# A two-layer recurrent and attention trunk: another order of the last feed-forward outputs and of the attention's blocks, with packed weights

## The chip, the cores and the metric

The kernel runs on one core of a Trainium2 chip. The time is the device time of one execution in microseconds (us). Three runs of the kernel before gave a median of 1279.37 us, from 1278.56 to 1281.68. Engines go by the names of the profile: PE (matrix products), DVE (VectorE), ACT (ScalarE), POOL (GpSimd) and SP (SyncE, which issues nearly all transfers).

## What is computed

One inference step of a trunk with two layers, over 512 prompt tokens and 64 sample tokens (8 sequences of 8), width 1024, feed-forward width 2816, all in fp32. Layer 0 is a gated recurrence, layer 1 a sliding-window attention with sinks; keys and values are computed once between them. Cut to what matters:

```python
def trunk(x, c, p0, conv_bufs, h0s, k_prev, v_prev, params):
    ...
    for l in range(DEPTH):
        sh1, sc1, g1, sh2, sc2, g2 = ada_mod(c, ada_w[l], ada_b[l], 6)
        h = modulate(rms_norm(x, norm_g[l, 0]), sh1, sc1)
        if l < N_A_LAYERS:
            out, nbuf, h_last = recurrent_block(h, rnn_w_in[l], rnn_conv_w[l], ...)
        else:
            q = apply_partial_rope((h @ attn_w_q[j]).reshape(B, T, N_HEADS, HEAD_DIM), pos)
            out = sliding_sink_attention(q, k_all, v_all, attn_sinks[j], p0) @ attn_w_o[j]
        x = x + g1[:, None, :] * out
        h = modulate(rms_norm(x, norm_g[l, 1]), sh2, sc2)
        x = x + g2[:, None, :] * swiglu(h, ffn_w_in[l], ffn_w_out[l])
        if l == N_A_LAYERS - 1:
            kv_shift, kv_scale = ada_mod(c, kv_ada_w, kv_ada_b, 2)
            hk = modulate(rms_norm(x, kv_norm_g), kv_shift, kv_scale)
            kv = (hk @ w_kv).reshape(B, T, 2, N_KV_HEADS, HEAD_DIM)
            ...
    y = rms_norm(x, final_g)

# in recurrent_block / rg_lru: the gates, one 128x256 block for each 128 channels
g = jnp.einsum('btnc,ncd->btnd', xb, gate_w) + gate_b
```

## The kernel before

**Halves and products.** The tokens are cut into two halves, A and B in the order strings, h = 0 and 1 in the code: 256 prompt tokens and 32 sample tokens each, so HC = 288 columns (with gaps for the convolution, CW = 300). The stream of each half stays on chip as `x[0]`, `x[1]` (x0, x1 in the profile), the normalised operand of its products as `h` (h0x, h1x). Each fp32 product is made of three fp32r matmuls for each 128x128 block of weights: high part of the weights by high and by low part of the operand, and low part of the weights by high part (`product`). A matmul takes 288 columns.

**Weights.** A `Unit` is the weights of one 128-column output. SP loads it into a `raw` slot (four of 128x1024), and `convert` makes two `wh` slots of it: ACT copies the high part, DVE subtracts it from `raw` for the low part. There are ten `wh` slots, so five units at a time. `drop` gives a unit's slots back when both halves have used it (`left` counts down from 2).

**Layer 0.** The string RNN orders input products (x, y) and gates (g0 to g7), and half B runs behind half A. `gates` (L1043 on) splits the convolved channel block `sl` into a high part `ta` (ACT, COPY, shown as CAST) and a low part `tb` (L1049, on POOL), then does three matmuls of 300 columns for each of the two gate units into banks `mm`, and a chain of tanh, exp, sqrt and a scan on ACT, DVE and POOL follows. All weights of the modulations are multiplied in small steps strewn between (`ada`).

**Feed-forward.** `ffn` computes the 22 blocks of 128 middle channels in GROUPS of 6, 6, 6 and 4, and after each group adds that group's share of the output to the stream: `out` multiplies the group by one 128-column output m for one half, and `residual` adds it (a SCALAR_TENSOR_TENSOR for the prompt, and small operations for the samples), and after the last group squares it for the next norm. For the last group `emit` runs half B behind half A by LEAD outputs:

```python
                lead = LEAD if k == len(GROUPS) - 1 else 0
                for j in range(KC + lead):
                    for h, m in ((0, j), (1, j - lead)):
                        if 0 <= m < KC:
                            out(k, m, h)
```

When a half's eighth output is done, `after(h)` is recorded: in layer 0 the sum of squares over the partitions (six matmuls of one column into a bank, with `small` and `acc`), the inverse root (`tst`, then back over the columns into `acc`), and the normed and modulated operand `h` for keys and values; in layer 1 the final norm and the output.

**Keys, values, queries.** Between the layers stand four products for keys and values (`kvjobs`, m = 0 to 3), first all four for half A, then all four for half B. `kv_done` follows each half's fourth: it modulates the operand again for the queries, and for half B first converts two query units.

**Attention.** The string ATT sets the order of the jobs in layer 1: q, a, o are a query product, one attention chunk (two heads) over the half's 256 prompt tokens and an output product; s is one sample sequence, f ends a half. Its last letter is the half. A chunk's scores, softmax, transposes and products with the values are small PE instructions, with DVE, ACT and POOL between them; a query or output product is 24 matmuls.

**The order of instructions.** All of this is only recorded, each operation with a priority (its place in the record, moved by a few `early` biases). `schedule` then builds the order of every engine by a greedy simulation with estimated costs and delays, and the program is written out in that order. So a change of one job moves rows elsewhere too. As all operations are written from one line, all instructions bear L447, and the profile tells them apart by their tiles.

Of the kernel before, what the change touches and what calls it, by code (L numbers as in the profile page):

```python
# [16 lines left out]
ALU = mybir.AluOpType  # L17
AX = mybir.AxisListType

P = 128  # L20
D = 1024
KC = D // P
# [5 lines left out]
HC = 288  # L28
CW = 300
# [1 line left out]
EPS = 1e-6  # L31
SLOT = 304
LAG = 7
LEAD = 4
NHI = 5
ADA, ADA2 = 1.6, 0.95
AB = 4
# [10 lines left out]
MQ = "4 V VVG SSSV VG"  # L48
# [1 line left out]
WIN = 600  # L50

RNN = "x0 x1 x2 g0 g1 x3 y0 y1 x4 g2 g3 x5 y2 x6 y3 g4 g5 x7 y4 y5 g6 g7 y7 y6"
ATT = ("q0A q1A a0A q0B q2A a1A q1B a0B q3A a2A q2B a1B q4A a3A q3B a2B q5A a4A q4B a3B q6A a5A q5B a4B q7A a6A s0A q6B a5B s1A "
       "a7A s2A q7B s3A s0B a6B fA s1B o0A s2B a7B s3B o1A fB o2A")
LOOK = {"PE": 24, "DVE": 24, "ACT": 24, "POOL": 24, "SP": 24}
NRAW = 4
NSL, NTA, NTB, NTD = 37, 7, 8, 4
# [2 lines left out]
SH1, SC1, G1, SH2, SC2, G2 = range(6)  # L60
KVSH, KVSC = 6, 7
L1 = 8
# [411 lines left out]
def trunk_kernel(ctx, tc, a):  # L474
# [93 lines left out]

    xt = [None] * 5

    ALL = slice(0, P)

    def x_load(t):
        xt[t] = regs()
# [346 lines left out]
    def modulated_h(h, gsc, gsh, how, xn=None, known=False):  # L921
        H[h] = hkind[h](F32R)
        modulated(h, gsc, gsh, how, xn=xn, known=known)
# [6 lines left out]
    class Unit:  # L930
        def __init__(self, kc, srcs):
            self.kc, self.srcs, self.raw, self.hi, self.lo = kc, srcs, None, None, None
            self.left = 2

    units = []
    nload, nconv = [0], [0]
# [2 lines left out]
    def load_more(upto=NRAW):  # L939
        while nload[0] < len(units) and nload[0] - nconv[0] < upto:  # L940
            u = units[nload[0]]
            u.raw = raws()
            t = u.raw.f[:, 0 : u.kc * P].rearrange("p (k n) -> p k n", n=P)
            for rows, ks, cols, src in u.srcs:
                Q.dma_start(t[rows, ks, cols], src)
            nload[0] += 1
# [21 lines left out]
    def unit_cols(w, c0, k0=0, kc=KC):  # L968
        src = w[k0 * P : (k0 + kc) * P, c0 : c0 + P].rearrange("(k p) n -> p k n", p=P)
        u = Unit(kc, [(ALL, slice(0, kc), ALL, src)])  # L970
        units.append(u)
        return u

    def product(o, u, ops, first=True, last=True):
        n = u.kc
        hi, lo = u.hi.r, u.lo.r
        for k in range(n):
            xh, xl = ops[k]
            ks = slice(k * P, (k + 1) * P)
            T.matmul(o, hi[:, ks], xh, start=(first and k == 0), stop=False)  # L980
            T.matmul(o, hi[:, ks], xl, start=False, stop=False)
            T.matmul(o, lo[:, ks], xh, start=False, stop=(last and k == n - 1))
# [60 lines left out]
    def gates(c):  # L1043
        def run(h):
            s1 = RN[h][c]
            xc = s1.f[:, 0:CW]
            xh, xl = ta(F32R), tb(F32R)
            S.copy(xh.r[:, 0:CW], xc)
            G.tensor_tensor(xl.r[:, 0:CW], xc, xh.f[:, 0:CW], ALU.subtract)  # L1049
            ks = slice(c * P, (c + 1) * P)  # L1050
            os_ = []
            for u in ug:
# [116 lines left out]
    def ffn(l, g, after):  # L1169
# [24 lines left out]
        f0 = 0  # L1194
        for n in GROUPS:
            blocks.append([(unit_cols(wi, f * P), unit_cols(wi, DFF + f * P)) for f in range(max(f0, PLAIN), f0 + n)])
            outs.append((f0, [unit_cols(wo, m * P, f0, n) for m in range(KC)]))
            f0 += n
        pairs_ = [None] * PLAIN + [b for bs in blocks for b in bs]
        W = {}  # L1200
# [49 lines left out]
        def queue():  # L1250
            for k, bs in enumerate(blocks):
                for i in range(max(PLAIN, sum(GROUPS[:k])), sum(GROUPS[: k + 1])):
                    st = steps(i)
                    if i == PLAIN:
                        nxt = steps(i + 1)
                        for s_, names in ((st, ("11", "12")), (nxt, ("11", "12")), (st, ("22", "S1", "S2", "S3", "S4")), (nxt, ("22", "S1", "S2", "S3", "S4"))):
                            for n in names:
                                todo.append((1, s_[n]))
                    elif i > PLAIN + 1:
                        for n in ("11", "22", "S1", "S2", "12", "S3", "S4"):  # L1260
                            todo.append((1, st[n]))
                for _ in outs[k][1]:
                    todo.append((2, convert))

        def pump(want=lambda: True):
# [73 lines left out]
        def out(k, m, h):  # L1339
            f0, us = outs[k]  # L1340
            n, u = GROUPS[k], us[m]
            pump(lambda: u.hi is not None)
            o = ps()
            product(o[:, 0:HC], u, [(mid[h][f][0].r[:, 0:HC], mid[h][f][1].r[:, 0:HC]) for f in range(f0, f0 + n)])
            last = k == len(GROUPS) - 1
            residual(h, o, m, g, last)
            if last and l == 1:
                final_chunk(h, m)
            drop(u)
            pump()  # L1350
            if m == KC - 1:
                for f in range(f0, f0 + n):
                    for s_ in mid[h][f]:
                        s_.done()
                if last:
                    after(h)
# [143 lines left out]
        return f  # L1500

    def kv_done(h):
        if h == 1:
            convert()
            convert()
        modulated_h(h, L1 + SC1, L1 + SH1, MQ, XN[h], True)

    for m in range(4):
        linear(unit_cols(a["w_kv"], m * P), hops, evac_k(m) if m < 2 else evac_v(m - 2), kv_done if m == 3 else None)


    kvjobs, jobs = jobs, []
# [476 lines left out]
```

## Time and profile before

| what | value |
| --- | --- |
| median of the three runs | 1279.37 us |
| profiled execution | 1278.79 us |
| its span | 1277.0 us |
| DMA moved | 165.40 MB, 130 GB/s |
| POOL | 267.8 us (21%), 558 instructions |

The profiled execution is one run; its span is the time from its first to its last instruction, and 1.8 us lie around it. A busy PE is one that has a matmul running; weight loads (PEld) overlap with it. A windows row gives, for a stretch, each engine's busy time and number of instructions, the clock that PE was granted (1.00 is full) and the share and rate of the DMA. A timeline row gives the start in us and the length of a run of like instructions, and in brackets the idle time ahead of it on its engine, with what ended that.

### The profile page before, as it was taken

How to read it: one execution, taken by the hardware profiler on the slowest of the kernel's cores; microseconds unless marked ns; L12 is line 12 of the kernel's file. 1: busy time of each engine (PE TensorE's matmuls, PEld its weight loads, DVE VectorE, ACT ScalarE, POOL GpSimd, SP SyncE). 2: the span in 40 equal slices, each digit the busy share in tenths (PEclk: the TensorE clock that was granted, in tenths of full speed). 3: DMA queues.
4: the chain of work that ended last, by engine and by line, in shares of the span. 5: the costliest groups of instructions: out<-in, count | busy, mean ns of one | idle time of the engine just before them, and what ended most of it. 6: DMA issues, size and time to landing. Idle time of an engine off the chain costs nothing.

```text
span 1277.0 us, 25350 instructions
## 1 busy us (share of the span) xinstructions
PE 1246.2 (98%) x9532; PEld 1171.9 (92%) x9532; DVE 918.3 (72%) x2275; ACT 668.4 (52%) x1508; POOL 267.8 (21%) x558
## 2 busy tenths in 40 slices
PE   7999999999999999999989999999999999999997
PEld 5788899899999899899988987899999999999997
DVE  6988785895587468657579787448956965875767
ACT  4789873753255235414467678438543541552443
POOL 3476630100100011110133435100001001001012
PEclk9999999999999999999999999899999999999999
DMA  9956454535456654554342321233241342233222
GB/s 305 332 162 215 158 166 149 170 92 174 147 153 193 183 163 155 173 174 149 100 99 48 60 76 50 66 99 112 75 124 55 95 116 82 74 103 90 80 87 75
DMA packets 223982, 165.40 MB, mean 130 GB/s; under 512 B 23758, under 2 KB 209066, under 8 KB 223827
## 3 DMA queue, kind: packets, MB, share of 16 engines
q1 hardware_dynamic: 223410, 163.45, 42.5%
q8 instruction: 75, 1.23, 0.4%
q14 instruction: 49, 0.39, 0.1%
q0 software_dynamic: 448, 0.32, 0.1%
HBM read 160.85 MB, written 4.87 MB: 130 GB/s over the span
## 4 chain that ended last, share of the span: by engine, by line
PE 88%; DVE 7%; ACT 3%; issue 1%; POOL 0%; DMA 0%; ACTq 0%; SPq 0%; DVEq 0%; POOLq 0%
PE mm L447 84%; PE ada L447 4%; DVE sl L447 2%; DVE ta L447 1%; DVE wh L447 1%; DVE h L447 1%; ACT ta L447 1%; ACT L447 1%; DVE tb L447 1%; ACT h L447 1%; ACT sl L447 0%; ACT wh L447 0%; ACT tb L447 0%; DVE raw L447 0%; DVE td L447 0%
## 5 line engine op out<-in xcount | busy, mean ns | idle before, releaser
L447 PE MATMUL mm<-h,wh 128*128 128x288 f32 x4128 | 597.3, 298 | 8.7 <-ACT h L447 3.6
L447 PEld LDWEIGHTS mm<-h,wh 128*128 128x128 f32 x4128 | 561.8, 189 | 29.8 <-issue 10.4
L447 PE MATMUL mm<-sl,wh 128*128 128x288 f32 x3218 | 460.2, 296 | 0.8 <-ACT ta L447 0.8
L447 ACT CAST wh<-raw 128x512 fp32r<-128x512 f32 (+2 forms) x388 | 270.6, 710 | 357.3 <-PE mm L447 217.1
L447 PEld LDWEIGHTS mm<-sl,wh 128*128 128x128 f32 x3218 | 436.2, 188 | 8.9 <-issue 6.7
L447 DVE TENSOR_TENSOR wh<-raw,wh 128x512 fp32r<-128x512 f32 (+2 forms) x388 | 310.6, 812 | 59.2 <-ACT wh L447 57.1
L447 DVE SCALAR_TENSOR_TENSOR x<-mm,mods,x 128x256 f32<-128x256 f32 x160 | 77.1, 482 | 141.9 <-PE mm L447 141.7
L447 POOL TENSOR_TENSOR td<-td,td 128x288 f32<-128x288 f32 x38 | 35.6, 936 | 476.3 <-ACT td L447 468.2
L447 POOL TENSOR_TENSOR x<-x,ta 128x32 f32<-128x32 f32 x152 | 56.0, 368 | 343.2 <-DVE ta L447 343.1
L447 PE MATMUL mm<-tb,wh 128*128 128x288 f32 (+1 forms) x488 | 88.2, 296 | 2.6 <-POOL sl L447 1.6
L447 PEld LDWEIGHTS mm<-tb,wh 128*128 128x128 f32 x488 | 72.4, 188 | 4.5 <-POOL sl L447 1.9
L447 ACT COPY td<-mm 128x288 f32<-128x288 f32 (+2 forms) x140 | 48.7, 363 | 38.7 <-PE mm L447 18.7
L447 DVE TENSOR_TENSOR raw<-raw,raw 128x512 f32<-128x512 f32 x76 | 61.4, 808 | 0.9
L447 PE MATMUL mm<-ta,wh 128*128 128x288 f32 (+1 forms) x254 | 56.0, 298 | 0.0
L447 DVE TENSOR_TENSOR td<-mm,td 128x288 f32<-128x288 f32 x76 | 34.6, 455 | 27.6 <-PE mm L447 27.3
L447 DVE TENSOR_TENSOR raw<-raw 128x512 f32<-128x512 f32 x76 | 52.1, 687 | 1.1
L447 ACT ACTIVATE ta<-x 128x288 f32<-128x288 f32 x56 | 24.8, 444 | 51.6 <-POOL x L447 48.5
L447 PE MATMUL ada<-reg,cz 128*32 128x512 f32 (+1 forms) x448 | 50.3, 553 | 0.3
L447 PEld LDWEIGHTS mm<-ta,wh 128*128 128x128 f32 x254 | 41.5, 188 | 1.7 <-ACT wh L447 0.8
L447 ACT ACTIVATE ta<-ta,stat 128x256 f32<-128x256 f32 (+2 forms) x72 | 32.2, 471 | 17.3 <-DVE stat L447 17.2
L447 DVE TENSOR_TENSOR acc<-acc,ta 128x288 f32<-128x288 f32 x54 | 24.5, 453 | 11.3 <-ACT ta L447 11.3
L447 ACT ACT_TABLE_LOAD x24 | 30.8, 1283 | 3.4 <-DMA raw<-in_c_sample_dram 3.1
(202 smaller groups left out, 1212.7 us busy)
## 6 DMA issues: line engine op xcount, KB each, us to landing
raw<-in_ffn_w_in_dram SPq DMA_DIRECT2D x88, 512.0 KB
reg<-in_ada_w_dram SPq DMA_DIRECT2D x80, 512.0 KB
raw<-in_ffn_w_out_dram SPq DMA_DIRECT2D x48, 384.0 KB
raw<-in_rnn_w_in_dram SPq DMA_DIRECT2D x16, 512.0 KB
reg<-in_kv_ada_w_dram SPq DMA_DIRECT2D x16, 512.0 KB
wh<-in_ada_w_dram SPq DMA_DIRECT2D x24, 256.0 KB
raw<-in_rnn_w_out_dram SPq DMA_DIRECT2D x8, 512.0 KB
raw<-in_ffn_w_out_dram SPq DMA_DIRECT2D x16, 256.0 KB
```

The lines of the kernel that those rows point to most:

```text
L447: self.rec.add(eng, lambda: getattr(obj, name)(*map(real, args), **{k: real(v) for k, v in kw.items()}), cost, outs, ins, func, lat, port, ...
```

## The change

It has five parts. LEAD goes from 4 to 8, in both layers: the last group's eight outputs are all done for half A, then all for half B. The last group's weights (four blocks of 128 rows for an output) are packed by two outputs: `unit_two` loads four blocks of 256 columns into one `raw` slot, `product` picks the half of each block with `col`, and a unit is dropped after four uses; so eight units of 128x512 become four of 128x1024 in each layer. The low part in `gates` is subtracted on DVE instead of POOL (16 instructions). The query weights are converted after the second and the third key and value product of half B, one each, instead of two after the fourth. And ATT is another order of the same jobs. The matmuls are the same ones.

```diff
--- before
+++ changed
-LEAD = 4
+LEAD = 8
...
-ATT = ("q0A q1A a0A q0B q2A a1A q1B a0B q3A a2A q2B a1B q4A a3A q3B a2B q5A a4A q4B a3B q6A a5A q5B a4B q7A a6A s0A q6B a5B s1A "
-       "a7A s2A q7B s3A s0B a6B fA s1B o0A s2B a7B s3B o1A fB o2A")
+ATT = ("q0A a0A q1A q2A q0B a1A q1B a0B a2A q3A q2B a1B a3A q3B q4A q4B a2B q5A a4A a3B q6A a5A q5B a4B "
+       "q7A a6A q6B a5B s0A s1A a7A s2A s3A q7B s0B a6B fA a7B o0A s1B s2B o1A s3B o2A fB")
...
-    ALL = slice(0, P)
+    ALL, ALL2 = slice(0, P), slice(0, 2 * P)
...
             self.kc, self.srcs, self.raw, self.hi, self.lo = kc, srcs, None, None, None
-            self.left = 2
+            self.left, self.width = 2, P
...
-            t = u.raw.f[:, 0 : u.kc * P].rearrange("p (k n) -> p k n", n=P)
+            t = u.raw.f[:, 0 : u.kc * P].rearrange("p (k n) -> p k n", n=u.width)
...
-    def product(o, u, ops, first=True, last=True):
-        n = u.kc
+    def unit_two(w, c0, k0, kc):
+
+        src = w[k0 * P : (k0 + kc) * P, c0 : c0 + 2 * P].rearrange("(k p) n -> p k n", p=P)
+        u = Unit(2 * kc, [(ALL, slice(0, kc), ALL2, src)])
+        u.left, u.width = 4, 2 * P
+        units.append(u)
+        return u
+
+    def product(o, u, ops, first=True, last=True, col=0):
+        n = u.kc * P // u.width
         hi, lo = u.hi.r, u.lo.r
         for k in range(n):
             xh, xl = ops[k]
-            ks = slice(k * P, (k + 1) * P)
+            ks = slice(k * u.width + col, k * u.width + col + P)
...
             S.copy(xh.r[:, 0:CW], xc)
-            G.tensor_tensor(xl.r[:, 0:CW], xc, xh.f[:, 0:CW], ALU.subtract)
+            V.tensor_tensor(xl.r[:, 0:CW], xc, xh.f[:, 0:CW], ALU.subtract)
...
-            outs.append((f0, [unit_cols(wo, m * P, f0, n) for m in range(KC)]))
+            if n <= 4:
+                two = [unit_two(wo, m * P, f0, n) for m in range(0, KC, 2)]
+                outs.append((f0, [two[m // 2] for m in range(KC)]))
+            else:
+                outs.append((f0, [unit_cols(wo, m * P, f0, n) for m in range(KC)]))
...
-                for _ in outs[k][1]:
+                for _ in {id(u) for u in outs[k][1]}:
                     todo.append((2, convert))
...
-            product(o[:, 0:HC], u, [...])
+            product(o[:, 0:HC], u, [...], col=P * (m % 2) if u.width > P else 0)
...
     def kv_done(h):
+        modulated_h(h, L1 + SC1, L1 + SH1, MQ, XN[h], True)
+
+    def ahead_q(h):
         if h == 1:
             convert()
-            convert()
-        modulated_h(h, L1 + SC1, L1 + SH1, MQ, XN[h], True)
 
     for m in range(4):
-        linear(unit_cols(a["w_kv"], m * P), hops, evac_k(m) if m < 2 else evac_v(m - 2), kv_done if m == 3 else None)
+        linear(unit_cols(a["w_kv"], m * P), hops, evac_k(m) if m < 2 else evac_v(m - 2), (None, ahead_q, ahead_q, kv_done)[m])
```

**The gates on PE, layer 0.** The first place is PE where half A's block 6 and its neighbours are done: `mm74` and `mm75` are the two gate banks of one block, `ta63` its high part, `tb47` its low part, `wh19` and `wh21` the high weights, and `h11` the operand of half B's input product. Before:

```order
L447 MATMUL mm74_2127<-ta63_1848,wh19_719 128x300
L447 MATMUL mm74_2127<-ta63_1848,wh20_819 128x300
L447 MATMUL mm75_2132<-ta63_1848,wh21_775 128x300
L447 MATMUL mm75_2132<-ta63_1848,wh22_857 128x300
L447 MATMUL mm76_2139<-h11_441,wh39_1835 128x288 x2
L447 MATMUL mm76_2139<-h11_441,wh40_1851 128x288
```

Eighteen rows of the `h11` product and of another block's gates stand between, and then:

```order
L447 MATMUL mm79_2198<-ta67_2084,wh19_719 128x300
L447 MATMUL mm79_2198<-ta67_2084,wh20_819 128x300
L447 MATMUL mm74_2127<-tb47_2184,wh19_719 128x300
L447 MATMUL mm75_2132<-tb47_2184,wh21_775 128x300
L447 MATMUL mm80_2208<-ta67_2084,wh21_775 128x300
L447 MATMUL mm80_2208<-ta67_2084,wh22_857 128x300
```

With the change:

```order
L447 MATMUL mm74_2129<-ta63_1855,wh19_719 128x300
L447 MATMUL mm74_2129<-ta63_1855,wh20_819 128x300
L447 MATMUL mm74_2129<-tb47_1878,wh19_719 128x300
L447 MATMUL mm75_2137<-ta63_1855,wh21_775 128x300
L447 MATMUL mm75_2137<-ta63_1855,wh22_857 128x300
L447 MATMUL mm75_2137<-tb47_1878,wh21_775 128x300
L447 MATMUL mm76_2147<-h11_441,wh39_1840 128x288 x2
L447 MATMUL mm76_2147<-h11_441,wh40_1861 128x288
```

The matmuls with the low part `tb47` stood 24 and 23 rows behind the last with the high part; now they follow them at once, and the banks' product is complete before the next input product.

**The half norm on DVE, after layer 0's feed-forward.** Here `x0` and `x1` are the streams of the two halves, `mm` the outputs' banks, `tst0` the sums for half A's norm, `acc0` its inverse root, and `sl` and `tb` begin its operand for keys and values. Before:

```order
L447 TENSOR_SCALAR tst0_71<-mm249_8333 128x2
L447 TENSOR_SCALAR tst0_71<-mm249_8333 32x1
L447 SCALAR_TENSOR_TENSOR x1_65<-mm253_8319,mods_68,x1_65 128x256
L447 TENSOR_TENSOR acc1_70<-acc1_70,ta249_8343 128x288
L447 TENSOR_TENSOR ta250_8363<-mm253_8319,mods_68 128x32
L447 SCALAR_TENSOR_TENSOR x1_65<-mm254_8348,mods_68,x1_65 128x256
L447 TENSOR_TENSOR ta252_8387<-mm254_8348,mods_68 128x32
L447 TENSOR_TENSOR sl213_8395<-x0_64,acc0_69 128x128
L447 TENSOR_TENSOR sl205_8400<-x0_64,acc0_69 128x256
L447 TENSOR_TENSOR tb67_8405<-sl213_8395,mods_68 128x128
L447 TENSOR_TENSOR sl206_8407<-x0_64,acc0_69 128x256
```

With the change:

```order
L447 TENSOR_SCALAR tst0_71<-mm246_8234 128x2
L447 TENSOR_SCALAR tst0_71<-mm246_8234 32x1
L447 SCALAR_TENSOR_TENSOR x1_65<-mm249_8220,mods_68,x1_65 128x256
L447 TENSOR_TENSOR ta242_8253<-mm249_8220,mods_68 128x32
L447 TENSOR_TENSOR acc1_70<-acc1_70,ta243_8262 128x288
L447 TENSOR_TENSOR sl213_8273<-x0_64,acc0_69 128x128
L447 TENSOR_TENSOR sl205_8276<-x0_64,acc0_69 128x256
L447 TENSOR_TENSOR tb67_8281<-sl213_8273,mods_68 128x128
L447 TENSOR_TENSOR sl206_8286<-x0_64,acc0_69 128x256
L447 TENSOR_TENSOR tb67_8281<-tb67_8281,mods_68 128x128
L447 TENSOR_TENSOR sl208_8295<-x0_64,acc0_69 128x256
```

The first rows of half A's norm (`sl213`) stood behind the seventh of half B's eight outputs (mm254); now they stand behind its second (mm249), and the other six, from mm250 on, follow the norm.

**The end of the attention on PE.** Here `td` and `wh277` (`wh269`) are the last sample products of half B, `mm368` their bank; `h05` and `h15` are the operands of the output products for halves A and B, `mm400` and `mm402` (before) or `mm400` (changed) banks of half A and `mm399` on of half B; `ada392` is a chunk's product with the values. Before:

```order
L447 MATMUL ada392_10851<-td120_10759,sl224_8648 64x128 x2
L447 MATMUL ada392_10851<-td121_10761,sl225_8876 64x128 x2
L447 MATMUL ada392_10851<-td122_10768,sl225_8876 64x128 x2
L447 MATMUL ada392_10851<-td123_10772,sl226_8813 64x128 x2
L447 MATMUL mm402_10866<-h05_10059,wh308_10795 128x288 x2
L447 MATMUL mm368_10549<-td124_10869,reg109_9632 128x64 x2
L447 MATMUL mm368_10549<-wh277_9769,reg107_7879 128x256 x2
L447 MATMUL mm399_10886<-h15_10319,wh300_9903 128x288
L447 MATMUL mm401_10888<-h15_10319,wh302_9968 128x288
L447 MATMUL mm403_10890<-h15_10319,wh304_10133 128x288
L447 MATMUL mm405_10892<-h15_10319,wh306_10356 128x288
L447 MATMUL mm407_10895<-h15_10319,wh308_10795 128x288
```

With the change:

```order
L447 MATMUL mm368_10588<-td123_10797,reg109_9686 128x64 x2
L447 MATMUL mm368_10588<-td124_10808,reg109_9686 128x64 x2
L447 MATMUL mm368_10588<-wh269_9720,reg107_7879 128x256 x2
L447 MATMUL mm400_10792<-h05_10033,wh299_10583 128x288
L447 MATMUL mm400_10792<-h05_10033,wh298_10533 128x288 x2
L447 MATMUL mm400_10792<-h05_10033,wh299_10583 128x288
L447 MATMUL mm400_10792<-h05_10033,wh298_10533 128x288 x2
L447 MATMUL mm400_10792<-h05_10033,wh299_10583 128x288
L447 MATMUL mm400_10792<-h05_10033,wh298_10533 128x288 x2
L447 MATMUL mm400_10792<-h05_10033,wh299_10583 128x288
L447 MATMUL mm399_10843<-h15_10346,wh292_9780 128x288
L447 MATMUL mm400_10792<-h05_10033,wh298_10533 128x288 x2
```

Between the last sample product and the first matmul with `h15` stood nothing; now ten matmuls of half A's output (mm400) stand there.

2 lines of the change are left out of this document (1 added, 1 removed).

## The prediction

> **What bounds the kernel now.** I read the page's busy shares first, then its chain of work, then stretches of 32 us.
>
> ```profile
> PE 1246.2 (98%) x9532; PEld 1171.9 (92%) x9532; DVE 918.3 (72%) x2275; ACT 668.4 (52%) x1508; POOL 267.8 (21%) x558
> PE 88%; DVE 7%; ACT 3%; issue 1%; POOL 0%; DMA 0%; ACTq 0%; SPq 0%; DVEq 0%; POOLq 0%
> ```
>
> TensorE has a matmul running for 98% of the span and carries 88% of the chain that ended last; the other engines carry it where PE waits for them. The change leaves the matmuls alone, so all it can win is PE's idle time and PE's slow time.
>
> ```profile
> 448.00:480.00 32.00, 32.00 (x245) 30.40 (x244) 21.74 (x44) 10.76 (x21) 4.21 (x8) 1.00 0.52 164
> ...
> 640.00:672.00 32.00, 28.56 (x205) 26.80 (x204) 24.92 (x69) 21.83 (x47) 12.57 (x19) 1.00 0.43 100
> 672.00:704.00 32.00, 29.43 (x213) 27.91 (x213) 28.72 (x77) 22.70 (x56) 13.09 (x16) 1.00 0.29 59
> ...
> 768.00:800.00 32.00, 29.57 (x249) 23.05 (x249) 23.33 (x110) 26.51 (x99) 18.98 (x46) 1.00 0.20 60
> 800.00:832.00 32.00, 29.58 (x208) 27.11 (x209) 13.88 (x57) 12.30 (x42) 3.34 (x9) 0.84 0.25 72
> ...
> 1248.00:1277.00 29.00, 22.03 (x169) 20.57 (x167) 21.27 (x80) 9.61 (x19) 6.24 (x14) 0.90 0.24 83
> sum 1277.00, PE 1246.23 PEld 1171.95 DVE 918.27 ACT 668.37 POOL 267.79; mean PE 31.16 PEld 29.30 DVE 22.96 ACT 16.71 POOL 6.69
> ```
>
> The sum leaves 1277.0 - 1246.2 = 30.8 us of PE idle. A full stretch, 448 to 480, does 245 matmuls in 32 us: 0.131 us each, my price for a row of PE. Three stretches that the change touches are not full: keys and values (640 to 704) lack 3.4 + 2.6 = 6.0 us, and the attention's end (768 to 832) 2.4 + 2.4 = 4.8 us, with a clock of 0.84 in its last row. The tail lacks 7.0 us, and its last residual still waits for the same last matmul, so I leave it at nothing.
>
> **Gates: the low part goes from POOL to DVE.** These are the timeline rows around two late gates, and the groups of the operation moved and of its nearest kin on DVE.
>
> ```profile
> 152.07 1.05 POOL L447 COPY ta<-shT 128x4 f32<-128x4 f32 x1 [0.90 <-DVE ta L447]
> ...
> 153.94 0.81 POOL L447 TENSOR_TENSOR tb<-sl,ta 128x300 fp32r<-128x300 f32 x1
> ...
> 154.80 0.55 PE L447 MATMUL mm<-tb,wh 128*128 128x300 f32 x2 [1.64 <-POOL sl L447]
> ...
> 157.57 0.55 PE L447 MATMUL mm<-tb,wh 128*128 128x300 f32 x2 [0.37 <-POOL tb L447]
> ```
>
> ```profile
> L447 POOL TENSOR_TENSOR tb<-sl,ta 128x300 fp32r<-128x300 f32 x16 | 14.4, 910 | 0.0
> L447 DVE TENSOR_TENSOR sl<-sl,tb 128x300 f32<-128x300 f32 x16 | 8.4, 529 | 0.7 <-POOL tb L447 0.7
> ```
>
> PE stood 1.64 + 0.37 = 2.0 us for two low parts, as POOL worked through the chain of the gate before. In the new order on PE the low part follows the high part at once and stands on DVE, ahead of that chain. I take both waits as gone: **-2.0**. What DVE gets is 16 subtractions at 0.529 us, 8.5 us. They lie beside PE's products, as DVE has room:
>
> ```profile
> 64.00:160.00 96.00, 93.98 (x704) 83.68 (x703) 80.14 (x153) 84.01 (x158) 63.15 (x140) 1.00 0.55 178
> ```
>
> In these 96 us DVE is busy for 80.1; with 8.5 more it is at 88.6, or 92%. What is queued behind each subtraction on DVE is a weight's low part or a scan, and PE waits for the first. Bounds: at best also the 0.81 us that stand ahead of the first output product, -2.8; at worst all 8.5 us reach PE, 8.5 - 2.0 = +6.5. I stay near the best end, since the moved instruction ends earlier than before.
>
> ```profile
> 150.80 0.37 POOL L447 COPY ta<-shT 128x4 f32<-128x4 f32 x1 [1.99 <-DVE ta L447]
> ...
> 151.85 1.22 DVE L447 TENSOR_TENSOR wh<-raw,wh 128x1024 fp32r<-128x1024 f32 x1
> ```
>
> The same small copy on POOL takes 0.37 us alone and 1.05 us beside a DVE subtraction of 1.22 us. The Trainium skill, "SBUF — State Buffer", section "Who interferes with whom", says why: a DVE operation with two SBUF inputs takes a port pair that it shares with GpSimd, for its whole length. By that rule the move ends 16 such meetings of subtractions and opens 16 others with POOL's gate chain; the sum would stay where it is.
>
> **Keys and values: LEAD 8, and query weights earlier.** The waits of the two stretches, from the timeline:
>
> ```profile
> 658.44 1.70 PE L447 MATMUL mm<-h,wh 128*128 128x288 f32 x10 [1.08 <-ACT h L447]
> 660.29 0.66 PE L447 MATMUL mm<-h,wh 128*128 128x288 f32 x3
> ...
> 662.13 1.33 PE L447 MATMUL mm<-h,wh 128*128 128x288 f32 x8 [1.18 <-POOL h L447]
> ...
> 664.50 2.51 PE L447 MATMUL mm<-h,wh 128*128 128x288 f32 x16 [1.03 <-DVE wh L447]
> 666.84 0.69 PE L447 MATMUL mm<-small,acc 128*128 128x1 f32 x6
> ...
> 697.12 8.09 PE L447 MATMUL mm<-h,wh 128*128 128x288 f32 x59 [1.44 <-DVE wh L447]
> ```
>
> Half A's products wait 1.08 + 1.18 us for pieces of the normed operand h, and some 0.15 between (660.29). In the new order half A's sum of squares stands 46 rows earlier on PE, 46 x 0.131 = 6.0 us, while its first product stays where it was: there are now 76 rows between, for 33. DVE starts the norm behind half B's second output instead of its seventh. So these waits of 2.4 us go. What is late next is the low part of the second unit: 1.03 us of wait before, and now it stands behind six of half B's residuals.
>
> ```profile
> L447 DVE SCALAR_TENSOR_TENSOR x<-mm,mods,x 128x256 f32<-128x256 f32 x160 | 77.1, 482 | 141.9 <-PE mm L447 141.7
> ```
>
> ```profile
> 656.32 0.70 DVE L447 TENSOR_TENSOR sl<-x,acc 128x128 f32<-128x128 f32 x2
> ...
> 661.03 0.45 DVE L447 TENSOR_TENSOR acc<-acc,ta 128x288 f32<-128x288 f32 x1
> ...
> 661.80 0.18 DVE L447 TENSOR_TENSOR ta<-mm,mods 128x32 f32<-128x32 f32 x1
> ...
> 662.68 1.76 DVE L447 TENSOR_TENSOR wh<-raw,wh 128x1024 fp32r<-128x1024 f32 x1
> 664.37 0.41 DVE L447 TENSOR_TENSOR h<-tb,h 128x256 fp32r<-128x256 f32 x1
> ```
>
> The norm took DVE from 656.32 to 664.8, with a low part of 1.76 and one residual (0.48 + 0.18 + 0.45) among it; moved up by 6.0 it begins near 650.3, and without those its first 18 rows end near 656. The six residuals (6 x 0.48, 6 x 0.18, and three additions of squares of 0.45 ahead of the low part: 5.3, a little less as they overlap) end near 661, and the low part of 1.2 to 1.8 us near 662.3; PE, 25 rows into keys and values that begin at 657.4, wants it at 660.7. I take a wait of 1.5, 0.5 more than before. Half B's own waits are what is left, 6.0 - 2.4 - 1.0 - 1.4 = 1.1; its sum of squares comes earlier on PE and on DVE alike, so they stand. The 1.44 us at 697.12 are a wait for a query unit's low part: with two units converted ahead, in a stretch where DVE is otherwise busy 28.7 of 32 us, I take 1.0 of it. Sum -2.4 + 0.5 - 1.0 = **-2.9**. At best all 6.0 go. At worst the six unread outputs hold all six banks, and PE's next product, wanted at 657.4, waits for the first residual behind the norm; if the 18 rows end at 658.4 only, that is 1.0 + 0.48 + 0.18, some 1.7 us more: -1.2.
>
> **Attention: another order.** Here are four rows of the timeline, the last two from the stretch before the first, and three windows of 4 us.
>
> ```profile
> 806.93 3.46 PE L447 MATMUL mm<-h,wh 128*128 128x288 f32 x24
> ...
> 827.76 4.51 PE L447 MATMUL mm<-h,wh 128*128 128x288 f32 x22 [1.59 <-ACT h L447]
> ```
>
> ```profile
> 799.92 1.01 PE L447 MATMUL mm<-ident,reg 128*128 128x128 f32 x4 [0.56 <-PE mm L447]
> 801.24 0.48 PE L447 MATMUL mm<-ident,ta 128*128 128x128 f32 x1 [0.32 <-ACT tb L447]
> ```
>
> ```profile
> 800.00:804.00 4.00, 3.62 (x18) 2.75 (x20) 1.55 (x5) 2.51 (x11) 0.19 (x1) 0.50 0.55 157
> 804.00:808.00 4.00, 4.00 (x34) 3.54 (x32) 2.90 (x17) 1.62 (x7) 0.45 (x1) 0.64 0.46 132
> 828.00:832.00 4.00, 4.00 (x22) 4.00 (x23) 0.82 (x2) 0.00 (x0) 0.00 (x0) 0.66 0.45 131
> ```
>
> At 827.76 PE had waited 1.59 us for half B's operand, with nothing between the last sample product and that operand's first use. Now ten matmuls stand there: 10 x 0.131 = 1.3 of it is covered, and more follow interleaved, so I take -1.6 with the rest. The 22 matmuls behind took 4.51 us, for 22 x 0.131 = 2.9: the clock was 0.66 in that window. With the gap gone I take that as gone too, -1.6. Before 806.93 the order held 88 rows without a large product; now it holds 49, so 44% of the idle 2.4 us of 768 to 800, -1.0. The dip at 800 I keep. Sum **-4.2**. At best all idle of 768 to 832 and both dips (2.3 + 1.6) go, -8.7; at worst the waits move and nothing is gained: 0. SP's loads bear on that end: the fourth sample of a half loads its cache into the first one's buffer, and in the new order 25 rows of PE stand between the two uses, for 49. The rest of SP's queue keeps its order, at a DMA share of 0.2.
>
> The half clock at 800 came with gaps of 0.56 and 0.32 us and none longer. The Trainium skill, "TensorE: Matmul & The Clock Gate", section "What's actually happening", lets the clock fall only after an idle window of about 3.4 us; by it neither dip comes from one gap of 1.6 us, and covering the gap need not remove the dip.
>
> **Packing.** Each layer's eight conversions become four:
>
> ```profile
> L447 DVE TENSOR_TENSOR wh<-raw,wh 128x512 fp32r<-128x512 f32 x282 | 191.2, 694 | 46.7 <-ACT wh L447 45.3
> L447 DVE TENSOR_TENSOR wh<-raw,wh 128x1024 fp32r<-128x1024 f32 x58 | 72.7, 1255 | 9.3 <-ACT wh L447 8.7 <-issue 0.3
> ```
>
> That is 8 x 0.694 - 4 x 1.255 = 0.5 us of DVE in each layer, beside full PE windows: nothing. It holds eight of ten slots until half B is done; if that cover fails, the price is the wait for the second unit counted above.
>
> **Sum.** -2.0 - 2.9 - 4.2 = -9.1 on the profiled 1278.79, 0.6 under the median of the runs: **1269.7 us**.
>
> **Rivals.** (a) The attention's waits move: its chunks still need DVE and ACT (23.3 and 26.5 of 32 us busy in 768 to 800), and the new order puts two late query jobs side by side. Then 1278.79 - 4.9 = 1273.9. (b) DVE gives back what PE wins: the 8.5 us of subtractions reach PE in full, as ACT and DVE in 64 to 160 are both above 80 of 96. Then 1278.2, no change. Against it speaks the room of 8%. (c) Slower: in the recurrence each subtraction lands in the gate's chain on DVE and also holds a POOL operation of that chain by 1.05 - 0.37 = 0.68 us; 16 x (0.529 + 0.68) = 19.3, less the 9.1: 1289.0. It decides once 9.1 + 3.8 = 12.9 of the 19.3 reach PE, that is if DVE is above 95% in 64 to 160. (d) The clock falls at the end as before, although the gap is covered: 1269.7 + 1.6 = 1271.3.
>
> **How the numbers follow.** Forecast 0.48, (a) 0.17, (b) 0.17, (c) 0.09, (d) 0.09. The lower bounds -2.8 - 6.0 - 8.7 = -17.5 give 1261; (b) is the upper case, so the range ends at 1279 and leaves out (c). A measurement of this kernel tells about 0.3%, 3.8 us, from no change: faster is forecast, (a) and (d), 0.74; same is (b), 0.17; slower is (c), 0.09.
>
> **What would show it.** Right: no wait for POOL ahead of a tb matmul; PE idle in 640 to 704 near 3 us; no wait above 0.5 us for h at the attention's end, and a clock of 1.00 behind it. Wrong: PE idle in 64 to 160 above its 2.0 us with waits for DVE; a wait for a bank at the first key product; new waits for chunks in 704 to 800; or a stretch at half clock that is longer than the two of before.

## The result and the profile after

The changed kernel takes 1263.03 us (1262.14 to 1264.26, four runs), the one before 1280.53 (1278.56 to 1285.11, four runs): a ratio of 0.9873, 95% interval 0.9857 to 0.9889, so 14 to 18 us faster. The profiled execution is one of 1263.01 us with a span of 1261.2, 15.8 under the span before. From the page of the changed kernel, busy shares and the chain:

```profile
PE 1237.8 (98%) x9532; PEld 1166.9 (93%) x9532; DVE 920.3 (73%) x2283; ACT 663.1 (53%) x1498; POOL 252.7 (20%) x542
...
PE 86%; DVE 6%; ACT 4%; DMA 2%; POOL 1%; issue 1%; SPq 0%; ACTq 0%; DVEq 0%
```

PE still has the chain, with the same 9532 matmuls. Its idle time fell from 30.8 to 1261.2 - 1237.8 = 23.4, by 7.4; but its busy time fell too, by 8.4. So more than half of the gain is not idle time.

The stretches of 32 us that answer to those before (what PE, PEld, DVE, ACT and POOL were busy, the granted clock, the DMA):

```profile
640.00:672.00 32.00, 31.02 (x223) 29.17 (x222) 26.88 (x81) 22.25 (x52) 11.74 (x21) 1.00 0.16 35
672.00:704.00 32.00, 30.93 (x235) 29.77 (x234) 26.70 (x87) 23.30 (x60) 15.38 (x23) 1.00 0.34 73
768.00:800.00 32.00, 30.24 (x248) 24.33 (x248) 22.89 (x104) 25.00 (x98) 13.31 (x37) 1.00 0.33 93
800.00:832.00 32.00, 31.94 (x250) 30.66 (x249) 16.43 (x50) 11.26 (x29) 4.48 (x12) 1.00 0.30 87
```

All later work has moved forward by up to 16 us, so I cut both executions into stages at rows of PE that stand in both (each cut is the start of its row, but for the end of the last feed-forward matmul):

| stage, from the end of the one above to | before, us | after, us | difference |
| --- | --- | --- | --- |
| first gate matmul of 300 columns | 57.36 | 58.72 | +1.4 |
| half B's sum of squares after the recurrence | 182.60 | 179.82 | -2.8 |
| end of the last feed-forward matmul of layer 0 | 417.41 | 416.04 | -1.4 |
| last transpose of new values | 35.94 | 31.67 | -4.3 |
| half A's sum of squares after the attention | 166.61 | 157.32 | -9.3 |
| half B's | 17.91 | 17.94 | 0.0 |
| last sum of squares | 391.12 | 390.98 | -0.1 |
| end | 8.05 | 8.71 | +0.7 |

The first row is no work of the change: over the fourteen profiles of this study the first stage took 57.4 to 60.4 us, whatever the kernel, so its 1.4 us are chance, here against the change. The third row goes with the gates: the seven profiles with their low part on DVE took 416.0 to 416.4 us there, the seven without it 416.9 to 419.1. Why a stage behind the gates should do so stays open. The recurrence, the keys and values and the attention carry the rest of the result.

### The profile page after: what moved, and what is told of

Same layout as the page of the kernel before. It is cut to its first block, busy times and chain, and to the rows that moved or that the text cites. A ratio compares the mean times of both kernels' runs of the same rounds, so it can differ in the third digit from the quotient of the medians.

```text
span 1261.2 us, 25276 instructions
## 1 busy us (share of the span) xinstructions
PE 1237.8 (98%) x9532; PEld 1166.9 (93%) x9532; DVE 920.3 (73%) x2283; ACT 663.1 (53%) x1498; POOL 252.7 (20%) x542
## 4 chain that ended last, share of the span: by engine, by line
PE 86%; DVE 6%; ACT 4%; DMA 2%; POOL 1%; issue 1%; SPq 0%; ACTq 0%; DVEq 0%
PE mm L447 82%; PE ada L447 4%; DVE wh L447 1%; DVE ta L447 1%; ACT tb L447 1%; DVE sl L447 1%; ACT ta L447 1%; DVE tb L447 1%; ACT h L447 1%; DMA raw<-in_rnn_w_in_dram 1%; ACT wh L447 1%; POOL h L447 1%; DMA reg<-in_ada_w_dram 1%; ACT sl L447 1%; DMA reg<-in_x_prompt_dram 1%
## 5 line engine op out<-in xcount | busy, mean ns | idle before, releaser
L447 ACT COPY td<-mm 128x288 f32<-128x288 f32 (+2 forms) x140 | 49.0, 364 | 37.7 <-DVE mm L447 18.0
L447 DVE TENSOR_TENSOR td<-mm,td 128x288 f32<-128x288 f32 x76 | 34.5, 454 | 23.4 <-PE mm L447 23.3
L447 ACT ACTIVATE ta<-ta,stat 128x128 f32<-128x128 f32 (+2 forms) x72 | 32.3, 471 | 18.5 <-DVE stat L447 17.7
L447 ACT CAST sl<-ta 128x288 fp32r<-128x288 f32 x54 | 23.0, 431 | 18.5 <-DVE ta L447 18.5
```

What stands on the lines that cost most here:

```text
L447: self.rec.add(eng, lambda: getattr(obj, name)(*map(real, args), **{k: real(v) for k, v in kw.items()}), cost, outs, ins, func, lat, port, ...
```

## The experiments

Every kernel was timed against the one before, on one chip with the others of its group. First the parts, each alone in the kernel before.

**The attention's order alone**: `ATT` as changed, all else as before.

> The kernel before with the new attention order alone. Places theory (each part acts at its own place, and the attention's gain is idle time plus both half-clock stretches): about 9 us faster (8 to 10.5), no PE clock below 0.95 between 700 and 850 us. Prediction's theory (the gap at the end and one of the two stretches): 4.2 us faster, the first stretch at half clock stays. Joint theory (the attention gains only if the keys and values end earlier): less than 3 us faster.

1273.26 us, ratio 0.9955 (0.9943 to 0.9968): 5.8 us faster, between the first two theories. No stretch at half clock between 700 and 850 us; the stage took 158.3 us for 166.6, so 8.3 less, as the first theory has it. In this profile the first stage and layer 0's feed-forward stage each took 1.7 us more than in the one before, so only 4.8 of the 8.3 are left in the span.

**LEAD 8 and packing alone.**

```diff
-LEAD = 4
+LEAD = 8
...
+                two = [unit_two(wo, m * P, f0, n) for m in range(0, KC, 2)]
```

> The kernel before with LEAD 8 and the packed last group alone. Places theory: PE's waits for h at half A's keys and values go (2.3 us) and half B's shrink (1.0), 2 to 4 us faster, and the attention's two half-clock stretches stay. Prediction's theory: 1.9 us faster. Joint theory: over 5 us faster, as the attention starts with other engines further ahead.

1276.41 us, 0.9978 (0.9969 to 0.9987): 2.8 us faster. PE idle in 640 to 704 us fell from 6.0 to 2.2:

```profile
640.00:672.00 32.00, 30.85 (x225) 29.38 (x224) 26.52 (x80) 19.54 (x45) 11.69 (x22) 1.00 0.16 34
672.00:704.00 32.00, 30.99 (x227) 29.70 (x225) 25.62 (x71) 25.16 (x56) 13.74 (x16) 1.00 0.39 73
```

The stage of keys and values took 31.8 us, as in the whole change (31.7), so this part alone makes that stage. A half-clock stretch was left in the attention, one of 3.4 us.

**The gates' low part on DVE alone.**

```diff
-            G.tensor_tensor(xl.r[:, 0:CW], xc, xh.f[:, 0:CW], ALU.subtract)
+            V.tensor_tensor(xl.r[:, 0:CW], xc, xh.f[:, 0:CW], ALU.subtract)
```

> The kernel before with the gates' low part on DVE alone. Places theory and the prediction: PE's idle time between 64 and 192 us falls from 2.8 to about 0.4, so 2.0 to 2.5 us faster. Rival (DVE gives it back): no change, 0 to 1 us, and PE idle of 2 us or more for DVE's low parts in that stretch.

1275.17 us, 0.9976 (0.9966 to 0.9985): 3.1 us faster, and the recurrence took 179.8 us for 182.6, as in the whole change. All seven profiles with the low part on DVE took 179.8 to 179.9 us for it, the seven others 182.5 to 182.7. Its windows:

```profile
64.00:160.00 96.00, 96.00 (x723) 87.74 (x722) 82.03 (x168) 83.50 (x159) 47.95 (x123) 1.00 0.56 180
160.00:192.00 32.00, 31.60 (x236) 29.45 (x235) 27.73 (x61) 21.54 (x37) 17.14 (x36) 1.00 0.56 180
```

PE is full from 64 to 160, and DVE is at 82.0 of 96 us only. The rival falls.

**Query conversions ahead alone.**

```diff
     def kv_done(h):
-        if h == 1:
-            convert()
-            convert()
...
+    def ahead_q(h):
+        if h == 1:
+            convert()
```

> The kernel before with the two query conversions moved ahead alone. Prediction: the wait of 1.44 us for a query unit's low part shrinks by 1.0. Places theory: by 0.4, as the wait of 1.02 us in the changed kernel is the same one; both are near what these runs can tell, so the profile's row decides. Rival: the two conversions sit in front of half B's norm work on ACT and DVE and half B's waits grow by as much: no gain in PE idle between 640 and 704 us.

1278.48 us, 0.9992 (0.9983 to 1.0001): not told from no change. In the profile the wait of 1.44 us is gone altogether (PE idle in 640 to 704 is 4.5 for 6.0), and half B's waits are what they were. So the moved conversions do their work; in the whole change another order of the queries brings 1.02 us of the wait back.

Next, where in the attention the gain lies. Both orders hold the same jobs up to a4B, and the same from q7A on, so head and tail can be exchanged.

**New head, old tail:** the order starts `q0A a0A q1A q2A q0B a1A ...` and ends as before.

> The kernel before with the new attention order up to the job a4B, and the old order from q7A on. Places theory (the gain lies where the old order had its sparse stretch and its half-clock stretches, from 784 us on): 0 to 1.5 us faster, and half-clock stretches (1.7 us lost for each 3.4) in 780 to 835 us remain. Spread theory (the gain is that all chunks are spaced better): 3 to 4 us faster.

**Old head, new tail:** the order ends `q7A a6A q6B a5B s0A s1A a7A s2A s3A q7B s0B a6B fA a7B o0A s1B s2B o1A s3B o2A fB`.

> The kernel before with the old attention order up to a4B, and the new order from q7A on. Places theory: nearly all of the 5.8 us that the whole new order gave, 4.5 to 6.5 us faster, and no half clock in 700 to 850 us. Spread theory: 2 to 3 us faster.

**The last jobs of the end alone.** The edit moves more than the two jobs of the expectation: `a7B` and `o0A` go ahead of `s1B`, `o1A` ahead of `s3B`, and `o2A` ahead of `fB`.

```diff
-... fA s1B o0A s2B a7B s3B o1A fB o2A
+... fA a7B o0A s1B s2B o1A s3B o2A fB
```

> The kernel before with two jobs of the attention's end moved alone: a7B and o0A ahead of s1B, so that nine matmuls of half A's outputs stand between the last sample product and half B's first output product. Prediction: the wait of 1.59 us for h goes (to 0.4 or less), the half-clock stretch behind it goes, and the one near 800 us stays: 1.3 to 3.2 us faster. Rival (the stretches at half clock do not hang on that gap but on where they fall in a sparse part): the wait goes, 1.2 to 1.6 us, and half-clock stretches still lose 1.7 to 5.1 us.

The new head alone gives 1272.84 us, 0.9952 (0.9937 to 0.9966); the new tail alone 1273.24, 0.9948 (0.9935 to 0.9962); the last jobs alone 1275.8, 0.9969 (0.9960 to 0.9979). So 6.1, 6.7 and 4.0 us, and 5.8 for head and tail together: by the times either half gives as much as the whole, and both theories on where the gain lies fall. In the attention's stage the head gives 8.4 us, the tail 5.7, and both together 8.3. The 4.0 of the last jobs are more than either of their theories allowed (3.2 at most), though the interval begins at 2.7. The waits for half B's operand and the clock are these: new head (timeline, and the stretch of 32 us), then the last jobs:

```profile
821.64 8.55 PE L447 MATMUL mm<-h,wh 128*128 128x288 f32 x61 [1.59 <-ACT h L447]
```

```profile
800.00:832.00 32.00, 30.27 (x243) 28.62 (x243) 15.70 (x52) 11.75 (x36) 3.05 (x9) 1.00 0.29 84
```

```profile
827.58 2.61 PE L447 MATMUL mm<-h,wh 128*128 128x288 f32 x15 [0.19 <-ACT h L447]
```

```profile
800.00:832.00 32.00, 30.69 (x225) 28.28 (x224) 13.63 (x52) 13.37 (x47) 4.39 (x13) 0.89 0.35 101
```

With the new head the gap of 1.59 us is still there, yet the clock stays full. With the last jobs moved the gap is gone (0.19) and the end is at full clock, but 6.8 us near 802 are at half. So the stretches at half clock do not belong to fixed places of the order. The five kernels with the old order say the same: one had half clock only near 799 us, one only near 824, one near 783 and 794, and two at the end and earlier.

**The whole change without its attention order.**

```diff
-ATT = ("q0A a0A q1A q2A ... o2A fB")
+ATT = ("q0A q1A a0A q0B ... fB o2A")
```

> The changed kernel with the old attention order. Additive theory (parts act each at its place): the other three parts alone, 2.8 + 3.1 + 0.6 = 6.5 us faster than before, and half clock is back in the attention. Joint theory (the attention's order gains more with the earlier keys and values): 4 us faster or more than 10, as the 16 us of the whole then divide otherwise.

1271.16 us, 0.9934 (0.9919 to 0.9948): 8.4 us faster than before, for 6.9 as the sum of the three parts measured alone (2.8 + 3.1 + 1.0). Within the intervals these three add. With the 5.8 of the attention alone the sum is 12.7, and the whole gave 16.3 (15.3 when timed again, below): 3 us more, at the edge of the intervals. The 3.5 us that the profile of the order alone lost in two stages that have nothing of the attention in them are as much, but whether its other runs lost them is not known.

**The changed kernel again, and with LEAD back at 4**, the packing kept:

> The changed kernel once more, so that the next two stand beside it: 1262 to 1264.5 us. The activity theory (a window of 3.4 us at half clock follows one in which PE had less than about half of its time in full products, and the new order leaves few such windows) expects at most one half-clock window in 700 to 850 us; the chance theory (the order has nothing to do with it) expects two or three, as in the profiles of the old order.

```diff
-LEAD = 8
+LEAD = 4
```

> The changed kernel with LEAD back at 4, so that of this part only the packing is left. Places theory: the stage of keys and values, 31.7 us between the last feed-forward product and the last transpose of values, is back near 35.8, the tail from the last sum of squares on back from 8.7 near 8.1, and the time 2.5 to 4 us longer than the changed kernel's. Rival (the packing is what pays): the stage stays below 33 us, and the time within 1 us of the changed kernel's.

The changed kernel gave 1263.69 us, 0.9880 (0.9864 to 0.9896), with one window at half clock in the attention, whose stage took 158.0. With LEAD 4 it was 1267.15, 0.9914 (0.9899 to 0.9929): 3.5 us more, and the waits at the keys and values are back:

```profile
658.29 0.50 PE L447 MATMUL mm<-h,wh 128*128 128x288 f32 x2 [0.96 <-DVE ta L447]
659.65 0.61 PE L447 MATMUL mm<-h,wh 128*128 128x288 f32 x1 [0.86 <-ACT h L447]
660.67 4.69 PE L447 MATMUL mm<-h,wh 128*128 128x288 f32 x18 [0.41 <-POOL h L447]
```

That stage took 37.7 us, with 6.8 us at half clock in it. So LEAD pays and the packing does not. By the code the packing makes LEAD 8 possible, as eight unpacked units would need sixteen `wh` slots, and there are ten; LEAD 8 without it was not run. The tail took 9.2 us, not 8.1: that part of the expectation missed.

**Two versions built on this:** LEAD 8 in layer 0 alone, and with it a third query unit converted ahead.

```diff
-                lead = LEAD if k == len(GROUPS) - 1 else 0
+                lead = (LEAD if l == 0 else 4) if k == len(GROUPS) - 1 else 0
```

> The changed kernel with LEAD 8 in layer 0 and 4 in layer 1. Places theory: the tail, 8.7 us with LEAD 8 in both and 8.1 with 4, gives 0.6 us back and nothing else moves: 0.3 to 1 us faster than the changed kernel, at the edge of what the runs can tell, so the tail in the profile decides. Rival (the longer tail came from elsewhere): tail still 8.5 to 9.2 us.

```diff
-... (None, ahead_q, ahead_q, kv_done)[m])
+... (ahead_q, ahead_q, ahead_q, kv_done)[m])
```

> As the kernel with LEAD 8 in layer 0 alone, and three query units converted ahead, after the first, second and third key and value product of half B. Places theory: PE's wait for a query unit's low part, 1.02 us in the changed kernel, falls below 0.4, so some 0.6 us more than the layer 0 kernel, 1 to 1.5 us faster than the changed kernel. Rival (DVE is the bound there, busy for nearly all of the stretch): the wait only moves to half B's norm or to a later product, no gain.

1262.26 us, 0.9867 (0.9850 to 0.9885), and 1262.67, 0.9870 (0.9854 to 0.9886). Both intervals overlap with those of the changed kernel, so neither is shown to beat it. The tail of the first took 9.4 us, more than either theory had: taken from the row of the last sum it moves as that row is placed, while the last two stages together took 399.05 to 399.95 us in every kernel here. LEAD 8 in layer 1 costs nothing that these runs show. With three units ahead the query wait went (PE waits 0.75 us for a transpose of values in its place), and no time can be told from it.

## Where the attention's time went

For each profile, the attention's stage, its PE idle time (from the windows view over the stage) and its time at half clock:

```
kernel                 order      stage us   PE idle   half clock
before                 old         166.6       6.6       10.2
LEAD, packing          old         164.6       6.0        3.4
gates                  old         164.8       7.4        3.4
query conversions      old         165.2       5.0       10.2
without new order      old         164.7       5.8        6.8
last jobs              old, end    163.4       4.9        6.8
new tail               half        161.0       3.0        6.8
new head               half        158.2       4.8        0.0
order alone            new         158.3       3.9        0.0
changed                new         157.3       3.3        0.0
changed, again         new         158.0       2.9        3.4
LEAD 4                 new         159.1       2.6        6.8
LEAD 8 in layer 0      new         157.3       3.4        0.0
three units ahead      new         156.7       1.5        3.4
```

With the old order the stage took 165.2 us on average (five profiles), with the new 157.8 (six), and no old one is below a new one. Of the 7.4 us, 6.15 - 2.92 = 3.2 are idle time. The half clock fell from 6.8 to 2.3 us on average; it is not gone, as three of the six with the new order still have 3.4 or 6.8 us of it, between 786 and 799 us.

Half clock comes in lengths of 3.41 us and their multiples, and within a run all of its edges lie on one grid of 3.41 us. In the fourteen attention stages 630 whole windows of that grid ran at full clock. In 556 of them PE was busy for 3.2 us or more, and none was followed by half clock; in 74 it was busy for less, and 14 of these were. So half clock came only behind a window that PE did not fill, and behind few of those. These are windows of the grid, each with the one behind it. First come two pairs of the kernel before, then one of the gates alone and one of the change without its order; the second pair and these two lie around the same gap of 1.59 us at the attention's end. Last is another pair of the gates alone:

```profile
796.62:800.03 3.41, 2.85 (x19) 2.00 (x18) 1.46 (x8) 2.55 (x12) 0.95 (x3) 1.00 0.63 191
800.03:803.44 3.41, 3.03 (x14) 2.23 (x15) 1.28 (x4) 2.19 (x10) 0.19 (x1) 0.50 0.57 162
823.92:827.34 3.42, 2.26 (x18) 1.55 (x12) 1.56 (x6) 1.16 (x5) 0.25 (x1) 1.00 0.00 0
827.34:830.75 3.41, 2.98 (x12) 2.99 (x13) 1.48 (x2) 0.37 (x1) 0.00 (x0) 0.50 0.21 59
```

```profile
821.04:824.45 3.41, 1.83 (x11) 1.27 (x10) 2.14 (x5) 0.83 (x3) 0.00 (x0) 1.00 0.00 0
824.45:827.86 3.41, 3.41 (x16) 3.41 (x15) 0.00 (x0) 0.00 (x0) 0.00 (x0) 0.50 0.52 154
```

```profile
817.56:820.98 3.42, 1.83 (x13) 1.67 (x13) 2.12 (x4) 0.83 (x3) 0.00 (x0) 1.00 0.00 0
820.98:824.39 3.41, 3.41 (x27) 3.41 (x27) 0.58 (x2) 0.85 (x1) 0.06 (x1) 1.00 0.52 154
```

```profile
797.14:800.56 3.42, 1.77 (x14) 1.33 (x14) 2.01 (x6) 2.67 (x12) 0.71 (x4) 1.00 0.63 189
800.56:803.97 3.41, 3.41 (x39) 3.19 (x40) 2.67 (x17) 1.75 (x8) 0.45 (x1) 1.00 0.25 69
```

And where PE's large products (288 or 300 columns) began in the pairs from 821.04 and from 817.56 (timelines of the gates' kernel and of the other):

```profile
823.33 5.95 PE L447 MATMUL mm<-h,wh 128*128 128x288 f32 x30 [1.58 <-ACT h L447]
```

```profile
819.19 2.98 PE L447 MATMUL mm<-h,wh 128*128 128x288 f32 x19 [1.59 <-ACT h L447]
```

The windows from 821.04 and from 817.56 are equally busy, 1.83 us. But in the one the large products fill the last 824.45 - 823.33 = 1.1 us, in the other 820.98 - 819.19 = 1.8; behind the one the clock is 0.50, behind the other 1.00. Where a window holds large products and next to nothing else, half of it does seem to be the limit: over the fourteen traces, the two such windows with up to 1.75 us of them were followed by half clock, and of the forty-one with 1.77 to 2.45 us one was (2.09 us, with LEAD 4). Where small matmuls fill the window no limit shows. The window from 796.62 is 2.85 / 3.41 = 84% busy with 19 small matmuls, and half clock follows; the last pair above, from 797.14, begins with 14 small ones in 1.77 us, and full clock follows. Where the grid falls differs from run to run, so a gap of this size costs clock in some runs and not in others. All of this is read from windows, not tested by a kernel of its own, and what decides among the windows of small matmuls stays open.

The stage can also be added up from the distances between the starts of PE's matmuls. A kind is a shape with its tiles; for each pair of kinds, one behind the other, I take the 20th percentile of the distance over all fourteen profiles as its usual price, and sort what is above it. The stage before is then 129.1 us of usual distances, 5.6 of excess at half clock (gaps in it included), 7.6 in gaps over 0.3 us and 24.3 in shorter ones; after it is 127.4, 0.0, 5.6 and 24.3. So the 9.3 us between the two profiles are 5.6 of half clock, 2.0 of gaps, and 1.7 from cheaper neighbours: small matmuls among products instead of after each other. As averages, the five profiles of the old order have 129.2, 4.0, 7.3 and 24.7 us and the six of the new 127.6, 1.3, 5.1 and 23.8, so the 7.4 us are 2.7 of half clock, 2.2 of gaps and 2.5 of shorter distances.

The excess at half clock is no price of the clock by itself. Without the query wait, which the other parts of the change move, the two profiles of the old order with three windows at half clock took 165.2 us on average, the two with one 163.8: 0.7 us for a window, and not the 1.7 that half speed would cost a full PE. With that price the clock is worth some 0.9 of the 7.4 us, an estimate, and the rest is the order's other waits and distances. How the 7.4 divide is therefore not settled; that the order gives them is.

## Why the prediction was right, and where it was short

The three places and the direction held; 1263.0 lies in the range, 6.7 us under the forecast. By stages of the two profiles, more than forecast came from the gates (0.8), the feed-forward stage behind them (1.4), keys and values (2.4) and the attention with the query wait (4.1), less 1.4 in the first stage and 0.6 behind the attention. So the number was closer than its terms, as the first stage's chance hid 1.4 of the shortfall. By its steps:

- **Gates, -2.0 forecast, -2.8 in the stage.** Right, at the best bound: both waits for POOL are gone, the 0.81 ahead of the first output product (`sl`, x18) is gone too, and 0.34 stands ahead of a later one. First the row of the 0.81 before, then the changed kernel (timelines of PE):

```profile
166.15 2.65 PE L447 MATMUL mm<-sl,wh 128*128 128x288 f32 x18 [0.81 <-ACT ta L447]
```

```profile
161.19 0.44 PE L447 MATMUL mm<-ta,wh 128*128 128x300 f32 x2
161.46 0.30 PE L447 MATMUL mm<-tb,wh 128*128 128x300 f32 x1
...
163.96 2.65 PE L447 MATMUL mm<-sl,wh 128*128 128x288 f32 x18
...
171.38 0.79 PE L447 MATMUL mm<-sl,wh 128*128 128x288 f32 x4 [0.34 <-ACT sl L447]
```

  DVE was to reach 88.6 of 96 us and reached 82.1. The group rows show a part of why, two of the changed kernel and then the second of them before:

```profile
L447 DVE TENSOR_TENSOR tb<-sl,ta 128x300 fp32r<-128x300 f32 x16 | 7.5, 478 | 0.4 <-ACT ta L447 0.4
L447 DVE SCALAR_TENSOR_TENSOR sl<-td,vecT,sl 128x300 f32<-128x300 f32 x48 | 25.4, 544 | 0.9 <-ACT sl L447 0.3
```

```profile
L447 DVE SCALAR_TENSOR_TENSOR sl<-td,vecT,sl 128x300 f32<-128x300 f32 x48 | 26.8, 582 | 3.5 <-ACT sl L447 3.2
```

  The subtraction took 0.478 us, not 0.529, and its neighbours got shorter (this one was 582 ns before; the eight groups of 300 columns that DVE had before, this one among them, went from 80.4 to 77.7 us). So 2.7 of the 7.5 us came back on DVE. POOL's own groups of that width went both ways, from 16.4 to 18.9 and from 11.5 to 8.3 us. By the Trainium skill, "SBUF — State Buffer", section "Who interferes with whom", a DVE operation with two SBUF inputs and a GpSimd operation that reads SBUF exclude each other; the rows agree with that in kind, but no run here isolates it. The prediction's figure for it was misread: the copy that took 0.37 us was not alone, as DVE's timeline before has no gap beside it:

```profile
150.65 0.47 DVE L447 SCALAR_TENSOR_TENSOR ta<-ta,sl 128x300 f32<-128x300 f32 x1
151.03 0.53 DVE L447 SCALAR_TENSOR_TENSOR sl<-td,vecT,sl 128x300 f32<-128x300 f32 x1
```

  So the 0.68 us a meeting in rival (c) is a difference between two meetings, and not the price of one.

- **Keys and values, -2.9 forecast, -4.3 in the stage and -0.4 behind it.** Half A's waits of 2.4 us went, and the bank wait of the worst bound never came (the row at 692.87 is the query wait, behind the stage's end at 686.25):

```profile
654.42 6.85 PE L447 MATMUL mm<-h,wh 128*128 128x288 f32 x43
...
667.49 0.55 PE L447 MATMUL mm<-ident,ta 128*128 128x128 f32 x3 [0.80 <-ACT ta L447]
...
692.87 6.77 PE L447 MATMUL mm<-h,wh 128*128 128x288 f32 x49 [1.02 <-DVE wh L447]
```

  43 products stand in one row with no idle time that the timeline shows, so the added wait of 0.5 for the second unit's low part was wrong in sign. The old wait of 1.03 did not go altogether: the 43 starts, up to the next row at 661.11, take 6.7 us, where 43 x 0.131 is 5.6, and 0.46 of the difference stands where PE waits for that low part, for 1.3 by the same count before. Half B's waits, left standing at 1.1, are down to 0.80, for a copy of values. The query wait gave 0.4, not 1.0. The two errors go opposite ways, and the low part's is the larger.

- **Attention, -4.2 forecast, -9.3 in the profile, -7.4 on average.** The mechanism was right and its size too small. The gap at the end is covered:

```profile
808.42 1.13 PE L447 MATMUL mm<-wh,reg 32*128 32x256 f32 x4
809.48 5.74 PE L447 MATMUL mm<-h,wh 128*128 128x288 f32 x38
```

  The step that fell short is the sum of this part. "The dip at 800 I keep" took half clock as tied to a place, and the profiles show that it comes and goes from run to run, behind windows of the grid that PE does not fill. That both dips went in this profile, 10.2 us at half clock to none, is in part luck: near that place three of the six profiles of the new order still have one. The terms for idle time (1.6 + 1.0) were near the 3.2 measured on average. The shorter distances between PE's matmuls, 2.5 us on average, had no term at all. The 2.3 that the best case puts on the first dip comes without a working.

- **Clock rule.** The Trainium skill, "TensorE: Matmul & The Clock Gate", section "What's actually happening", asks for an idle window of about 3.4 us before half clock. The length of 3.41 agrees; the cause does not: of the windows above those 54%, 66% and 84% busy were followed by half clock, and none was idle. The measurement decides, and rival (d), which rested on that rule, did not come: with the gap covered none of eight profiles had half clock behind it, with the gap kept three of six had.

- **Packing and tail, nothing forecast.** Packing gave nothing of its own, and the last two stages moved by 0.5 us, within the 0.9 in which all kernels here lie.

- **Rivals.** (a), (b) and (c) fall with the parts measured alone: the attention gains 5.8 us, the gates 3.1.

## What to carry to other kernels

A wait on the busiest engine can cost more than its length: where it leaves a stretch thin, the clock may halve for the next one, so here a sparse stretch is best priced as a chance (14 of 74 windows) of 3.4 us at half clock and not as a place. To fill it, spread the small operations among large products; it mattered less which half of the order was mended, as by the times either half gave the whole gain. A timeline row without idle time can still hide short waits: count the starts in it. And compare stages cut at rows that stand in both traces, over several profiles, before a difference of 2 us is given a cause.

## What was not expected of the hardware

Half clock in the first 40 us came to 3.4 us in some profiles and to 13.7 in others, though the first stage is the same work in all. The stage's length goes with it: 57.4 to 57.8 us with 3.4 at half clock, 58.2 to 59.2 with 6.8, 59.1 to 59.5 with 10.2, and 60.3 to 60.4 with 13.7. Whether the clock makes the stage longer or an emptier stage lowers the clock is not shown. The 417 us of feed-forward work in layer 0 varied by 3 us: 1.8 of these are two waits of 1.39 and 0.41 us in one profile, and the seven profiles with the gates' low part on DVE are all faster than the seven without, most of it with no idle time to show for it. What sets that pace stays open.
